# Start addresses in SBUF: 64 mod 512 for all against 0 mod 512 for most and 0, 32, 64 ... 480 for the split activations

## The chip, the cores and the metric

The kernel is one program on one NeuronCore of a Trainium2 chip. The metric is device time in microseconds (us) of one execution. Four compute engines matter: TensorE (PE in the profile; its weight loads are a row of their own, PEld), VectorE (DVE), ScalarE (ACT) and GpSimd (POOL). SyncE (SP) issues all of the kernel's transfers. Operands lie in SBUF, which has 128 partitions; an address is a byte offset in each partition, and a tile of 512 fp32 values takes 2048 bytes of it.

## The reference

One layer of a hybrid block on 512 latent tokens and 256 context tokens, model width 2048, all fp32:

```python
h = rmsnorm(x, g_norm1) * (1 + sc1) + sh1           # sc, sh, gt: c @ w_mod
lat_in, lat_gates = project_heads(h, w_in, ...)      # q, k, v of 4 GLA and 4 mLSTM heads, gates
ctx_in, _ = project_heads(hc, w_in, ...)             # k, v of the context
lat = scans in both directions, from the context's final states
x = x + gt1 * (concat(norm(gla) * silu(g), sigmoid(o) * norm(mlstm)) @ w_out)
h2 = rmsnorm(x, g_norm2) * (1 + sc2) + sh2
u_gate, u_val = split(h2 @ w_up)                     # 2048 -> 2 x 5504
x = x + gt2 * ((silu(conv3x3(u_gate)) * u_val) @ w_down)
out = rmsnorm(x, g_final)
```

## The kernel before, in words

All big products are done in three parts. `split` (L88) rounds an fp32 tile to a "high" tile of type float32r with ScalarE and takes the rest as a "low" tile with VectorE; `mm3` (L99) then issues three matmuls into one PSUM bank: high by high, high by low, low by high. Each matmul loads its 128 x 128 stationary operand anew, so the PE row and the PEld row of the profile have the same count.

The weights come by `load_split` (L155): a transfer of 256 rows by 512 columns into one of four `raw` buffers, then `split` into one of two `hi` and two `lo` buffers. Every 128 columns of such a buffer are 512 bytes, so all stationary slices of a buffer start at the same address mod 512.

The activations lie in 32 tiles of 512 columns, 16 high and 16 low ones, made by `acttile` (L136). They hold in turn the normed input (`hTh`, `hTl`), the merged heads (`yTh`, `yTl`), and the normed input of the MLP (`h2h`, `h2l`). The products of the MLP's middle layer lie in other tiles (`gh`, `gl`, L935), made in the pool `fp`.

The stages in order of time. First the modulation vectors and the first two heads (`project_first`, L308; the order of its matmuls is pinned). Then the heads, one after another (`project`, `gla`, `mlstm`): here the banks `a` get q and k with the weights stationary and 512 tokens moving (L269), v with 128 tokens stationary and 256 weight columns moving (L274), and the context's k and v with 384 weight columns moving (L279). Then the output gates (banks `ga`, L817), the output projection (`wo`, L867), and the MLP: `up_gate` and `up_val` (banks `ug`, `uv`) by blocks of 512 columns, and `down_block` (banks `dn`) between them, the last block as `dl` (L992) by halves of the tokens. `unit` (L169) issues `ga`, `wo`, `ug` and `uv`: for each pair of row blocks it goes over four column blocks, and for each over the two row blocks, with three matmuls each.

Every instruction's engine and order is set by the scheduling layer from the program; the change keeps the order of all engines as it is: 11423 rows on PE, 1868 on DVE, 1187 on ACT, 236 on POOL and 660 on SP are the same in both programs.

The pools are laid out one behind another in SBUF in the order in which they are opened, each tile padded to a multiple of 32 bytes, behind a scratch area for descriptors that GpSimd would generate (16384 bytes by default). Where that puts the operands of the large products, in bytes mod 512 of their start:

| tiles | before | after |
|---|---|---|
| `hi`, `lo` weights and the `raw` of pool `wraw` | 64 | 0 |
| `hTh`, `hTl`, `yTh`, `yTl`, `h2h`, `h2l` (32 tiles) | 64, all | 0 to 480 in steps of 32 |
| `gh`, `gl` | 160 | 0 |
| `hch`, `hcl` (split context, 1024 bytes each) | 0 | 0 |

After the change the high tiles of row blocks 0 to 15 start at 256, 320, 0, 64, 128, 192, 256, 320, 384, 416, 448, 480, 384, 416, 448 and 480, the low ones at 288, 352, 32, 96, 160, 224, 288, 352, 0, 32, 64, 96, 128, 160, 192 and 224 mod 512.

Of the kernel before, what the change touches and what calls it, by code (L numbers as in the profile page):

```python
# [11 lines left out]
F32 = mybir.dt.float32  # L12
# [6 lines left out]
P = 128  # L19
# [3 lines left out]
T = 512  # L23
# [17 lines left out]

# columns of the constants
C_ID, C_LS, C_US, C_SEG = (P * i for i in range(4))
# [26 lines left out]
def block_kernel(ctx: ExitStack, tc: tile.TileContext, a: dict, out: bass.AP):  # L70
# [32 lines left out]

# [1 line left out]
    keep = pool(ctx, "keep")  # L105
    cst = keep.tile([P, C_END], F32, name="cst")
    cols = keep.tile([P, 148], F32, name="cols")
    msk = keep.tile([P, len(LEVELS), P], U8, name="msk")
    csil = keep.tile([P, KT], F32, name="csil")
    modc = {n: keep.tile([P, KT], F32, name=f"mod{n}") for n in (2, 3, 4, 5)}  # L110
# [25 lines left out]
    def acttile(k, part, name):  # L136
        return actp.tile([P, T], F32R, name=name, tag=f"a{part}{k}")

    def rsqrt(v, t, o):
        """o = v ** -0.5 with one Newton step; t is scratch."""  # L140
        S.activation(t, v, AF.Ln)
        S.activation(o, t, AF.Exp, scale=-0.5)
        mul(t, o, o)
        mul(t, t, v)
        V.tensor_scalar(out=t, in0=t, scalar1=-0.5, scalar2=1.5, op0=ALU.mult, op1=ALU.add)
        mul(o, o, t)
# [3 lines left out]

# [1 line left out]
    fillers = []  # L152
# [16 lines left out]
    def unit(src, name, xh, xl, n=4):  # L169
        """n accumulators: transposed products of 128 n weight columns with all 512 tokens."""  # L170
        accs = [acc(f"{name}_{i}") for i in range(n)]
        for kp in range(KP):
            wh, wl = load_split(src[kp], f"{name}_{kp}", w=P * n)
            for i in range(n):
                for kk in range(2):
                    k = 2 * kp + kk
                    mm3(accs[i], wh[:, kk, P * i : P * i + P], wl[:, kk, P * i : P * i + P],
                        xh[k], xl[k], k == 0, k == KT - 1)
        return accs

# [1 line left out]
    def mod_load(region, n):  # L182
        """The weights of 256 columns of one region."""
        raws = []
        for q in range(4):
            raws.append((wraw if q == 3 else mraw).tile([P, 4, 256], F32, name=f"raw_m{region}_{n}_{q}", tag="raw"))
            nc.sync.dma_start(raws[q], a["w_mod1"][8 * region + n, q])
        return raws

    def mod_rows(region, n, raws):  # L190
        """[128, 256]: the products with c and c_ctx, each in four parts on four rows."""
        bank = psb(f"ps_m{region}_{n}")
# [10 lines left out]
    def mod_cols(region, n, bank, rows):  # L203
        """Their sums as columns of 128 entries, with what the norm and the modulation make of them."""
        pc = bank[:, 256:260].rearrange("p (b c) -> p b c", c=2)
# [12 lines left out]
    def mod_chunk(region, n, kp, parts):  # L218
        """256 rows of the 512 columns n of one region, weighed by c and added up on DVE and Pool."""
        name = f"m{region}_{n}_{kp}"  # L220
# [16 lines left out]
    def mod_end(region, n, parts):  # L237
        """The sums over the partitions: four columns of 128 entries."""
        po = parts[1]
# [9 lines left out]
    def mod_fillers(regions, lag):  # L249
        """The steps of these regions; a block's sums end lag steps after its last load."""  # L250
        for region in regions:
            for n in range(4):
                parts = []
                for kp in range(KP):
                    fillers.append(lambda r=region, n=n, kp=kp, p=parts: mod_chunk(r, n, kp, p))
                fillers.extend([lambda: None] * (lag - 1))
                fillers.append(lambda r=region, n=n, p=parts: mod_end(r, n, p))
# [3 lines left out]

# [1 line left out]
    def project_chunk(kp, wh, wl, o, g, first=0, last=KT - 1):  # L263
        """256 rows of w into bank g of a head: q, k, v of two token tiles (twice), k and v of a context tile (twice)."""
        ks = list(enumerate((2 * kp, 2 * kp + 1)))
# [17 lines left out]
    def project(h):  # L283
        """q, k transposed and v for the latent tokens, k and v for the context tokens."""
        banks = [acc(f"a{h}_{g}", BANKS[g]) for g in range(6)]
# [7 lines left out]
    def early_group(kp, g, w, sums):  # L293
        """One bank of head 1, whose sums stay in SBUF."""
        ps = psb(f"a1_{kp}_{g}", BANKS[g])
# [12 lines left out]
    def project_first():  # L308
        """Heads 0 and 1 while the modulation vectors come in."""
        banks = [acc(f"a0_{g}", BANKS[g]) for g in range(6)]  # L310
# [60 lines left out]

# [1 line left out]
    st_h = ExitStack()  # L373
    states = pool(st_h, "states")
    # rows 0-15: the low rank decay inputs, row 16: ones, rows 32-47: the mLSTM gates
    glr = states.tile([48, T + TC], F32, name="glr")
# [4 lines left out]
    negg = states.tile([36, T], F32, name="negg")  # L381
    bg = states.tile([36, 2], F32, name="bg")
    accp = pool(st_h, "accp")
# [4 lines left out]

    # head 1, first in the places of activations that come last, then of inputs that were used first
    EARLY = 4  # L390
# [33 lines left out]
    def stream_rstd(xs, o, name, n):  # L424
        """[128, n]: each token's 1 / rms, the same in all rows; xs are [128, 512], the tokens once or twice."""
        tot = xp.tile([P, T], F32, name=f"sq_{name}", tag="sqs")
# [44 lines left out]
    V.tensor_copy(msk, mskf)  # L471
    # decay inputs and gate inputs: 32 columns, partial sums over k = g mod 4 in four row groups
    V.memset(glr, 1.0)
# [19 lines left out]

# [1 line left out]
    st_2 = ExitStack()  # L495
# [33 lines left out]
    def finish(h, ob, ssq, yT):  # L529
        """Head norm, then transposed into the two channel tiles of the head."""  # L530
        var = wtile(f"var{h}", "st1", TJ)
# [14 lines left out]
    def gla(h, pair, qk, v, kn, vn, yT):  # L546
        wlr = wk.tile([17, 2, DK], F32, name=f"wlr{h}", tag="wlr")
        nc.sync.dma_start(wlr, a["w_lr"][h])
        # context: final states
        cla = ytile(13, f"cla{h}", (P, 2, CJ, DK))  # L550
# [24 lines left out]

        # latent: decays, cumulated within 128 tokens, and over all of them
        la = wtile(f"la{h}", "la", 2, T)
# [20 lines left out]

        # scores by levels: pairs of neighbouring spans of b tokens, both directions at once
        sc = wtile(f"sc{h}", "la", 2, TJ, P)  # L600
# [66 lines left out]
    def ml_gates():  # L667
        """Rows 0-3: forward, time as context, latent; rows 32-35: backward, time as latent, context."""
        W = T + TC
# [56 lines left out]
    def mlstm(h, _, qk, v, kn, vn, yT):  # L726
        hh = h - H
        q, k = qk
        # context: final states
        kt = ytile(15, f"kt{h}", (P, 2, CJ, DK))  # L730
# [5 lines left out]
        for d in range(2):  # L736
# [3 lines left out]
            S.copy(c0[:, d, :], ps)  # L740
        # latent
        qs = wtile(f"qs{h}", "tmp", 2, T)
# [67 lines left out]

# [1 line left out]
    st_3 = ExitStack()  # L812
# [12 lines left out]
    tc.keep_in_program_order(S.preload_act_table_set("natural_log_exp_and_others"))  # L825
# [1 line left out]
    yh, yl, x2 = [], [], []  # L827
# [10 lines left out]
    def square(k, sums, pl, tag, sl=slice(0, T)):  # L838
        """Adds the squares of x2[k] to the first of sums, or appends them for the last two."""
        n = sl.stop - sl.start  # L840
# [8 lines left out]
    def token_rstd(sums, pl, name, n=T):  # L849
        """[128, n] in PSUM: each token's 1 / rms, the same in all rows."""  # L850
        nj = n // P
# [36 lines left out]

# [1 line left out]
    fp = pool(ctx, "fp")  # L890
    tp = pool(ctx, "tp", 4)
    cwt = fp.tile([P, NF, 9], F32, name="cwt")
    cbt = fp.tile([P, NF], F32, name="cbt")
    nc.sync.dma_start(cwt, a["conv_w"])
# [70 lines left out]

# [1 line left out]
    tc.keep_in_program_order(S.preload_act_table_set("natural_log_exp_and_others"))  # L967
# [47 lines left out]
def arrange(x, c, ctx, c_ctx, w_mod, b_mod, g_norm1, g_norm2, w_in, gla_w_lr, gla_b_lr, mlstm_b_gate,  # L1015
            gla_g_norm, mlstm_g_norm, w_out, w_up, conv_w, conv_b, w_down, g_final):
    """The inputs in the layouts that the kernel reads: only moved, never computed with."""
    def col(v):
        return v.reshape(-1, P).T

    def blocks(w, n):
        """[K, n columns] -> [K / 256, 128, 2, n]."""
        return w.reshape(-1, 2, P, n).transpose(0, 2, 1, 3)
# [53 lines left out]
```

## Time and profile before

| | |
|---|---|
| median of 3 runs | 2644.12 us (2642.51 to 2647.18) |
| profiled execution, first to last instruction | 2643.6 us |
| PE busy | 2570.1 us, 12866 matmuls |
| PEld busy | 2136.7 us, 12866 loads |
| DVE, ACT, POOL busy | 1366.2, 860.2, 285.0 us |
| moved from and to HBM | 315.10 MB, 4.19 MB |

The profile has one execution, whose span is 2643.6 us; the profile gives no other time for it. Matmuls are pipelined: the duration of one in the profile (some 390 ns for 512 columns) is its way through the array, and overlaps with the next. What a matmul costs is the distance from its start to the start of the next, which is read from the chain that ended last (a length and a count) or from the starts in the timeline.

### The profile page before, as it was taken

The page shows a single profiled execution, that of the slowest core. Times are in us where ns is not written, and L with a number is a line of the kernel's source. Part 1 is how long each engine was busy: PE and PEld are TensorE (multiplying, and loading weights), DVE is VectorE, ACT ScalarE, POOL GpSimd, SP SyncE. Part 2 cuts the span into 40 slices and gives each one's busy share as a digit, 9 for nine tenths or more (in the row PEclk, how much of TensorE's full clock was granted, in tenths as well). Part 3 has the DMA queues.
Part 4 walks back from the last instruction along what each step waited for, and adds up shares of the span by engine and source line. Part 5 has one row for each costly group of instructions (what it writes and reads, how often), then busy time and mean ns, then how long its engine had stood idle before and what let it go on. Part 6 is the DMA issues. An engine that isn't in the chain of part 4 may idle for free.

```text
span 2643.6 us, 31995 instructions
## 1 busy us (share of the span) xinstructions
PE 2570.1 (97%) x12866; PEld 2136.7 (81%) x12866; DVE 1366.2 (52%) x1971; ACT 860.2 (33%) x1219; POOL 285.0 (11%) x255
## 2 busy tenths in 40 slices
PE   6999999999999999999999999999999999999998
PEld 4887888878987888887878888888888888888887
DVE  6656664554334465548686336533653365326534
ACT  4223433333323344334343123312331233123332
POOL 0002221302112232310331000000000000000001
PEclk9999999999999999999999999999999999999998
DMA  8750102213323566642554222222232223222323
GB/s 315 281 196 33 41 33 72 70 35 112 128 94 119 183 229 222 205 159 76 202 175 156 96 96 96 96 96 96 96 96 96 96 97 96 95 96 90 105 90 99
DMA packets 96348, 321.38 MB, mean 122 GB/s; under 512 B 10884, under 2 KB 15304, under 8 KB 96200
## 3 DMA queue, kind: packets, MB, share of 16 engines
q1 hardware_dynamic: 96200, 319.34, 35.4%
q8 instruction: 101, 1.65, 0.3%
q14 instruction: 47, 0.39, 0.0%
HBM read 315.10 MB, written 4.19 MB: 121 GB/s over the span
## 4 chain that ended last, share of the span: by engine, by line
PE 86%; DVE 7%; DMA 3%; ACT 2%; issue 2%; POOL 0%; SPq 0%; POOLq 0%; ACTq 0%; DVEq 0%
PE ug L95 17%; PE dn L95 17%; PE uv L95 16%; PE a L95 14%; PE wo L95 6%; PE ga L95 6%; DMA raw_m<-in_w_mod 2%; PE po L662 2%; PE po L782 1%; PE ps_m L95 1%; PE dl L95 1%; PE sl L631 1%; DVE ex L80 1%; DVE cv L924 1%; DVE ex L83 1%
## 5 line engine op out<-in xcount | busy, mean ns | idle before, releaser
L95 PE MATMUL ug<-h2h,hi_ug 128*128 128x512 f32 x688 | 269.0, 392 | 1.6 <-ACT h2h L883 1.6
L95 PE MATMUL uv<-h2h,hi_uv 128*128 128x512 f32 x688 | 268.7, 391 | 1.4 <-ACT hi_uv L89 1.4
L95 PE MATMUL uv<-h2h,lo_uv 128*128 128x512 f32 x688 | 268.6, 390 | 1.1 <-DVE lo_uv L90 1.1
L95 PE MATMUL ug<-h2h,lo_ug 128*128 128x512 f32 x688 | 268.6, 390 | 0.7 <-DVE lo_ug L90 0.7
L95 PE MATMUL ug<-h2l,hi_ug 128*128 128x512 f32 x688 | 268.6, 390 | 0.0
L95 PE MATMUL uv<-h2l,hi_uv 128*128 128x512 f32 x688 | 268.4, 390 | 0.0
L95 PE MATMUL dn<-gh,lo_d 128*128 128x512 f32 x644 | 256.9, 399 | 0.0
L95 PE MATMUL dn<-gl,hi_d 128*128 128x512 f32 x644 | 253.8, 394 | 0.0
L95 PE MATMUL dn<-gh,hi_d 128*128 128x512 f32 x644 | 252.5, 392 | 0.0
L924 DVE SCALAR_TENSOR_TENSOR cv<-pad,cwt,cv 128x512 f32<-128x512 f32 x344 | 242.2, 758 | 10.5 <-ACT cv L922 9.1
L233 POOL TENSOR_TENSOR sum_m<-sum_m,raw_m 128x512 f32<-128x512 f32 x112 | 174.2, 1555 | 552.4 <-ACT raw_m L232 304.8
L90 DVE TENSOR_TENSOR lo_ug<-raw_ug,hi_ug 128x1024 fp32r<-128x1024 f32 (+1 forms) x88 | 107.4, 1221 | 241.3 <-ACT hi_ug L89 241.3
L90 DVE TENSOR_TENSOR lo_uv<-raw_uv,hi_uv 128x1024 fp32r<-128x1024 f32 (+1 forms) x88 | 105.3, 1196 | 182.2 <-ACT hi_uv L89 181.8
L90 DVE TENSOR_TENSOR lo_d<-raw_d,hi_d 128x1024 fp32r<-128x1024 f32 x82 | 98.8, 1205 | 173.0 <-ACT hi_d L89 171.3
L231 DVE SCALAR_TENSOR_TENSOR sum_m<-raw_m,csil,sum_m 128x512 f32<-128x512 f32 x112 | 101.9, 910 | 151.8 <-DMA raw_m<-in_w_mod 148.1
L89 ACT CAST hi_d<-raw_d 128x1024 fp32r<-128x1024 f32 x82 | 84.9, 1035 | 291.2 <-PE dn L95 207.0
L89 ACT CAST hi_ug<-raw_ug 128x1024 fp32r<-128x1024 f32 (+1 forms) x88 | 90.8, 1032 | 267.8 <-PE ug L95 200.1
L89 ACT CAST hi_uv<-raw_uv 128x1024 fp32r<-128x1024 f32 (+1 forms) x88 | 90.9, 1033 | 254.7 <-PE uv L95 182.0
L95 PEld LDWEIGHTS uv<-h2h,lo_uv 128*128 128x128 f32 x688 | 129.6, 188 | 29.3 <-DVE lo_uv L90 2.3
L95 PEld LDWEIGHTS ug<-h2h,hi_ug 128*128 128x128 f32 x688 | 129.8, 189 | 29.0 <-ACT h2h L883 1.9
L95 PEld LDWEIGHTS uv<-h2h,hi_uv 128*128 128x128 f32 x688 | 129.4, 188 | 28.9 <-ACT hi_uv L89 1.8
L95 PEld LDWEIGHTS ug<-h2h,lo_ug 128*128 128x128 f32 x688 | 129.7, 189 | 28.3 <-DVE lo_ug L90 1.1
(310 smaller groups left out, 5277.6 us busy)
## 6 DMA issues: line engine op xcount, KB each, us to landing
raw_m<-in_w_mod SPq DMA_DIRECT2D x192, 512.0 KB, 4.3
raw_ug<-in_w_up SPq DMA_DIRECT2D x80, 512.0 KB, 3.2
raw_uv<-in_w_up SPq DMA_DIRECT2D x80, 512.0 KB, 3.2
raw_d<-in_w_down SPq DMA_DIRECT2D x79, 512.0 KB, 3.4
raw_h<-in_w_heads SPq DMA_DIRECT2D x64, 512.0 KB, 3.2
raw_ga<-in_w_gates SPq DMA_DIRECT2D x32, 512.0 KB, 3.7
raw_wo<-in_w_out SPq DMA_DIRECT2D x32, 512.0 KB, 3.7
xl<-in_xT SPq DMA_DIRECT2D x16, 256.0 KB, 5.4
```

The source lines that it names most:

```text
L80: V.tensor_tensor(out=o, in0=x, in1=y, op=ALU.subtract)
L83: V.tensor_tensor(out=o, in0=x, in1=y, op=ALU.mult)
L89: S.copy(hi, x)
L90: return V.tensor_tensor(out=lo, in0=x, in1=hi.bitcast(F32), op=ALU.subtract).ins
L95: ins = PE.matmul(*args, **kw)
L231: V.scalar_tensor_tensor(out=dv, in0=raw[:, 0, :], scalar=ce, in1=dv, op0=ALU.mult, op1=ALU.add)
L233: G.tensor_tensor(out=po, in0=po, in1=raw[:, 1, :], op=ALU.add)
L631: PE.matmul(ps[:, i, :], ex[:, 1, P * i : P * i + P], ex[:, 0, P * j : P * j + P], start=True, stop=True)
L662: PE.matmul(po, l, r, start=(n == 0), stop=(n == len(parts) - 1))
L782: PE.matmul(po, e[:, P * j - j0 : P * j - j0 + P], v[i], start=False, stop=(i == rng[-1]))
L924: V.scalar_tensor_tensor(out=t3, in0=src, scalar=w, in1=t3, op0=ALU.mult, op1=ALU.add)
```

## The change

The scratch area shrinks to 1024 bytes, and three small tiles (`csil`, `bg`, `cbt`) become longer, so that the tiles behind them start at multiples of 512 bytes. The 32 activation tiles become 2080 bytes long instead of 2048, of which 2048 are used as before, so that each starts 32 bytes further on, mod 512, than the one before it. The comments and doc strings that the diff also takes out do nothing and are left out here.

```diff
@@ block_kernel
-    csil = keep.tile([P, KT], F32, name="csil")
+    csil = keep.tile([P, 128], F32, name="csil")[:, 0:KT]
...
     def acttile(k, part, name):
-        return actp.tile([P, T], F32R, name=name, tag=f"a{part}{k}")
+        return actp.tile([P, T + 8], F32R, name=name, tag=f"a{part}{k}")[:, 0:T]
...
-    bg = states.tile([36, 2], F32, name="bg")
+    bg = states.tile([36, 24], F32, name="bg")[:, 0:2]
...
-    cbt = fp.tile([P, NF], F32, name="cbt")
+    cbt = fp.tile([P, 152], F32, name="cbt")[:, 0:NF]
@@ kernel
-    nc = bacc.Bacc("TRN2", target_bir_lowering=False, num_devices=1)
+    nc = bacc.Bacc("TRN2", target_bir_lowering=False, num_devices=1, dynamic_dma_scratch_size=1024)
```

## The prediction

> **What bounds the kernel now.** I read the page first (busy time, then the chain that ended last, as shares), then the chain in order of time, then the groups of instructions, and at last single matmuls in the timeline.
>
> ```profile
> span 2643.6 us, 31995 instructions
> PE 2570.1 (97%) x12866; PEld 2136.7 (81%) x12866; DVE 1366.2 (52%) x1971; ACT 860.2 (33%) x1219; POOL 285.0 (11%) x255
> ...
> PE 86%; DVE 7%; DMA 3%; ACT 2%; issue 2%; POOL 0%; SPq 0%; POOLq 0%; ACTq 0%; DVEq 0%
> ...
> raw_ug<-in_w_up SPq DMA_DIRECT2D x80, 512.0 KB, 3.2
> ```
>
> TensorE is busy for 97% of the span and is 86% of the chain, so the end moves with what a matmul costs. The chain in time shows that cost, block by block:
>
> ```profile
> 1510.00:2611.00 1101.00, 1101.00 (x4882) 905.91 (x4881) 513.34 (x623) 312.43 (x381) 0.00 (x0) 1.00 0.29 95
> ```
>
> ```profile
> 837.18 37.99 PE ga L95 x167
> ...
> 1123.69 43.63 PE wo L95 x192
> ...
> 1513.97 43.56 PE uv L95 x192
> 1557.54 43.52 PE ug L95 x192
> 1601.05 43.52 PE uv L95 x192
> 1644.57 43.52 PE ug L95 x192
> 1688.09 89.61 PE dn L95 x384
> ...
> 2593.47 17.88 PE dl L95 x149
> ```
>
> The first row is a window (length, then busy time and count of PE, PEld, DVE, ACT, POOL, clock, DMA): from 1510 to 2611 us PE is never idle, at a granted clock of 1.00, and DVE is busy for 513.34 of 1101 us. The chain rows (start, length, count) give the distance between matmuls: 43.52 / 192 = 226.7 ns in `ug` and `uv`, but 89.61 / 384 = 233.4 ns in `dn`, and 17.88 / 149 = 120.0 ns in `dl` with half as many columns. `ug` and `dn` run the same instruction at the same clock, three parts by `mm3`, 512 columns, with a weight load behind each start. What differs is where the operands begin: weights and activations both at 64 mod 512 in `ug`, the moving `gh` and `gl` at 160 against weights at 64 in `dn`. So 6.7 ns a matmul go with the address.
>
> How much can go with it at most? At half clock the same matmul shows no such loss:
>
> ```profile
> 1194.60:1199.28 4.68, 4.68 (x13) 3.62 (x12) 4.61 (x9) 1.63 (x2) 0.00 (x0) 0.50 0.00 0
> ```
>
> ```profile
> 1197.42 0.63 PE L95 MATMUL ug<-h2h,lo_ug 128*128 128x512 f32 x1
> 1197.84 0.63 PE L95 MATMUL ug<-h2h,hi_ug 128*128 128x512 f32 x1
> 1198.27 0.63 PE L95 MATMUL ug<-h2l,hi_ug 128*128 128x512 f32 x1
> ...
> 1513.81 0.40 PE L95 MATMUL uv<-h2h,hi_uv 128*128 128x512 f32 x1
> ...
> 1515.89 0.39 PE L95 MATMUL uv<-h2h,hi_uv 128*128 128x512 f32 x1
> 1516.12 0.39 PE L95 MATMUL uv<-h2l,hi_uv 128*128 128x512 f32 x1
> ```
>
> The first three starts, at clock 0.50, are 425 ns apart on average, half of which is 212.5 ns. At full clock a steady matmul takes 226.7, so some 14 ns are lost beside the stream of columns. The next rows are the first matmuls of `uv` behind a `dn` block: nine of them, from 1513.81 to 1515.89, take 2080 / 9 = 231.1 ns each, and only then does the distance become 226.7. I read this as two streams, the moving columns and the next weights, that need a few operations to settle into the order in which they disturb each other least; in `dn` they never reach it. It is a reading; the numbers stand without it.
>
> **The change part by part.** The order of instructions on each engine and on the queues of SP and POOL is unchanged, and so is every wait; only addresses move.
>
> Part 1, the smaller scratch area and the three longer small tiles. All transfers are issued on SP's queue (the issue row above names it), none by GpSimd, so nothing uses the scratch: no cost. What it does is to put weights, `raw`, `gh` and `gl` at 0 mod 512. For `dn` this makes moving and stationary starts equal, as they are in `ug` now, so I price a `dn` matmul at 226.7.
>
> ```profile
> L95 PE MATMUL dn<-gh,lo_d 128*128 128x512 f32 x644 | 256.9, 399 | 0.0
> L95 PE MATMUL ug<-h2h,hi_ug 128*128 128x512 f32 x688 | 269.0, 392 | 1.6 <-ACT h2h L883 1.6
> L95 PE MATMUL ga<-hTh,hi_ga 128*128 128x512 f32 x256 | 100.9, 394 | 0.0
> L95 PE MATMUL wo<-yTh,hi_wo 128*128 128x512 f32 x256 | 100.0, 391 | 0.0
> L95 PE MATMUL a<-hTh,hi_h 128*128 128x512 f32 x256 | 104.3, 408 | 2.4 <-ACT hTh L89 1.6 <-ACT qk L513 0.7
> ```
>
> Each count is one of the three parts of `mm3`. `dn` has 3 x 644 = 1932 matmuls, nearly all of them on the chain (its rows of 384 and its zero idle time): 1932 x 6.69 ns = 12.9 us less. Its ends are 0 (if the 233.4 has another cause) and 12.9.
>
> Part 2, the staggered activations. They are the moving operand of 3 x 688 in each of `ug` and `uv` (4128), 3 x 256 in each of `ga` and `wo` (1536) and 3 x 256 in `a` (768). These now start anywhere in steps of 32 against weights at 0. Which offsets cost? The rows give three: 0 (`ug`, 226.7), 96 (`dn`, 233.4), and 64, in the context's products of 384 columns (weights move at 64 mod 512, `hch` and `hcl` stand at 0):
>
> ```profile
> 297.05 0.34 PE L95 MATMUL a<-lo_h,hch 128*128 128x384 f32 x1
> ...
> 298.09 0.34 PE L95 MATMUL a<-lo_h,hch 128*128 128x384 f32 x1
> ```
>
> Six of them take 1040 / 6 = 173.3 ns; 384 columns at 212.5 / 512 ns are 159.4, so the loss is 14 ns, the same as at offset 0. With three points the plainest rule is that an even multiple of 32 costs as 0 does and an odd one as 96 does. By that rule one matmul in three is odd in row blocks 0 to 7 (high, low, high at a, a + 32, a), and one in two in blocks 8 to 15 (there both tiles of every second block are odd): 5/12 in the mean, 5/12 x 6.69 = 2.8 ns. Against it stands that the offset now changes from one matmul to the next, and that a changed sequence needs nine matmuls to settle: if it never settles, all pay the 231.1 of the unsettled nine, 4.4 ns more. I take the middle, 3.6 ns, with 2.8 and 4.4 as the forecast's own ends; the outer ends are 0 (it settles as now) and 6.7 (all pay as `dn`).
>
> How many lie on the path? `ug` and `uv` all (the window above has no idle PE, and before it they are the largest pieces), `ga` and `wo` all but a few gaps, and of `a` I count half, 384, since between the heads' steps PE waits for other engines and a slower matmul only eats idle time. 4128 + 1536 + 384 = 6048; x 3.6 ns = 21.8 us more.
>
> Part 3, the same tiles as stationary operands of the 256-column products of `a`, and `dl`, whose weights lie in activation tiles:
>
> ```profile
> 295.04 0.28 PE L95 MATMUL a<-lo_h,hTh 128*128 128x256 f32 x1
> ...
> 296.00 0.28 PE L95 MATMUL a<-hi_h,hTh 128*128 128x256 f32 x1
> ```
>
> Eight of them take 960 ns, 120.0 each at offset 0; `dl` takes 120.0 at offset 96. With 256 columns the offset costs nothing, so I put 0 here, with bounds of 3 ns either way on half of 3 x 512: 2 us.
>
> Part 4, everything else that moves: VectorE, ScalarE and GpSimd read and write the same tiles at other addresses. Were they slower by a tenth, DVE would still be busy for some 565 of the 1101 us above: the cover is its idle half, and it would have to go before the end moved. Transfers land at other offsets in SBUF; a load of 512 KB lands in 3.2 us, one of 256 KB in the row below in 2.6,
>
> ```profile
> raw_d<-in_w_down SPq DMA_DIRECT2D x3, 256.0 KB, 2.6
> ```
>
> so 64 bytes out of 4096 can be worth some 0.6 x 2 / 64 = 0.02 us a load, and DMA is 3% of the chain: under 1 us either way.
>
> Sum: -12.9 + 21.8 = +8.9 us, a span of 2652.5. The profiled execution's span lies 0.5 us under the median of the runs, 2644.12, so I predict 2653 us.
>
> [...]
>
> **The rivals.**
>
> A, not slower: the staggered streams settle as they do now, at 226.7, since the shift of 32 bytes is small against 2048, and only `dn` changes. 2644.1 - 12.9 = 2631 us. For it: offsets 0 and 64 both settle at a loss of 14 ns. Against it: the nine unsettled matmuls of `uv`. It decides from a price under 12.9 / 6048 = 2.1 ns on.
>
> B, the change does nothing: the pace depends on something else than addresses, such as the loop order of `down_block`; then both terms are 0 and the time is 2644 us. For it: only two stages are compared. Against it: the same instruction, clock and operand count in both. [...]
>
> C, worse: every staggered matmul pays the 6.7 ns of `dn`: 6048 x 6.69 = 40.5, less 12.9, is 2672 us; or the price is as forecast and `dn` keeps its 233.4, 2644.1 + 21.8 = 2666. For it: `dn` never settles at an odd offset.
>
> D, the stagger takes the collisions away: half of the 14 ns gone on 6048 matmuls is 42 us, with `dn` 55: 2589 us. For it: 14 ns are there to be had. Against it: no steady stage of this trace has lost less, at offsets 0, 64 or 96.
>
> **How the numbers follow.** About 0.2%, 5.3 us, is what a measurement of this kernel can tell from no change. Chances: the forecast 0.55 (from 6048 x 2.8 - 12.9 = +4.0 to 6048 x 4.4 - 12.9 = +13.7, so 2648 to 2658; 0.08 of it within 0.2%), A 0.17, B 0.08, C 0.15, D 0.05. Faster is A and D, 0.22; same B and the lower end of the forecast, 0.16; slower the rest, 0.62. The range takes in A with its 2 us of part 3 and C with the same on top: 2629 to 2676, leaving out D and what of C is worse than `dn`'s price.
>
> **What would show it.** In the chain after, `dn` rows of 384 should be 87.0 us (226.7 each), and `ug` and `uv` rows of 192 between 44.0 and 44.4; `dl` and the 256-column starts should stay at 120 ns. Rows of 43.5 mean A, `dn` rows still at 89.6 mean B or C's second form, rows over 44.8 C, rows under 43 D. The prediction is wrong if the price goes by more than the offset mod 64, or if a few misplaced matmuls set off a longer unsettled stretch than nine.

## The result, and the profile after

The changed kernel takes 2658.97 us in the median of 4 runs (2657.11 to 2660.06), the kernel before 2644.85 (2642.51 to 2647.18) beside it: a ratio of 1.0046, with a 95% interval of 1.0031 to 1.006. It is slower, by 0.3 to 0.6%. All times of the block here are of executions at a granted clock near 0.99; two far slower ones, one of `gh` moved below (4295.86 us at a clock of 0.556) and one of the kernel before (8361.22 us), are left out. The profiled execution has grown by 11.5 us, from 2643.6 to 2655.1.

The page of the kernel after (span, busy time, shares of the chain that ended last):

```profile
span 2655.1 us, 31995 instructions
PE 2584.2 (97%) x12866; PEld 2136.1 (80%) x12866; DVE 1362.3 (51%) x1971; ACT 861.0 (32%) x1219; POOL 283.6 (11%) x255
...
PE 86%; DVE 7%; DMA 2%; ACT 2%; issue 2%; POOL 0%; SPq 0%; POOLq 0%; ACTq 0%; DVEq 0%
```

TensorE is as busy a share as before, with the same 12866 matmuls in 14.1 us more. The chain of the kernel after in order of time (start, length, what, count):

```profile
836.70 38.81 PE ga L95 x167
...
1127.80 44.63 PE wo L95 x192
...
1519.60 44.53 PE uv L95 x192
1564.13 44.54 PE ug L95 x192
...
1697.75 87.08 PE dn L95 x384
...
2605.47 17.64 PE dl L95 x149
```

`dn` has fallen to 87.08 / 384 = 226.8 ns a matmul, what `ug` took before. `ug` and `uv` have risen from 226.7 to 44.54 / 192 = 232.0, and `wo` by the same (44.63 against 43.63 us for 192). `dl`, with 256 columns, went from 120.0 to 118.4.

Where the 11.5 us arose is read by laying the starts of the same steps side by side. Two pairs of rows are missing for it, the sums of the norm ahead of the MLP (`ps_rms`) and the first block of the MLP; here is the same view of the kernel before,

```profile
1186.16 2.41 PE ps_rms L855 x20
...
1193.84 46.56 PE ug L95 x192
```

and of the kernel after:

```profile
1191.60 3.93 PE ps_rms L855 x20
...
1200.81 47.09 PE ug L95 x192
```

| stretch, by the starts of its rows | before, us | after, us | difference |
|---|---|---|---|
| start to the first long row of `ga` | 837.18 | 836.70 | -0.48 |
| from there to the first `ug` (gates, output projection) | 356.66 | 364.11 | +7.45 |
| from there to the `uv` behind the first `dn` | 320.13 | 318.79 | -1.34 |
| from there to `dl` (steady MLP) | 1079.50 | 1085.87 | +6.37 |
| from there to the end | 50.13 | 49.63 | -0.50 |

In the steady MLP the paces give the difference: the rows there count 3168 matmuls of `ug` and `uv` at +5.31 ns (+16.8 us) and 1548 of `dn` at -6.59 (-10.2). In the two stretches ahead of it the granted clock has a part. From the first long row of `ga` to the last start of `wo` the kernel takes 5.9 us more (346.98 and 352.92), where 1536 matmuls at +5.2 ns would give 8.0; the other 1.5 us of the 7.45 lie behind `wo`, where the clock had already dropped when `ps_rms` ran: its 20 matmuls took 3.93 us at a clock of 0.58 after, and 2.41 at 1.00 before.

From the first `ug` to the `uv` behind the first `dn` the paces would give 960 x 5.31 - 2.5 = +2.6 us, and the stretch became 1.3 shorter, 3.9 less than that. Windows at half clock make up some half of it (length, busy time and count of PE, clock, share and GB/s of the DMA), before

```profile
1193.84:1199.70 5.86, 5.86 (x14) 0.50 0.00 0
1366.90:1370.30 3.40, 3.40 (x9) 0.51 0.80 239
```

and after:

```profile
1200.81:1205.80 4.99, 4.99 (x12) 0.50 0.00 0
```

At half clock a matmul takes 425 ns in place of 227 or 232, so 9.3 us of it against 5.0 are some 2.0 us. Whether the change has to do with this stays open: of all the traces, the second of these windows is missing in those with steps of 32 and 64 and in that of `gh` moved alone, and is there in the others. The rest, some 1.9 us, are for the most part waits of PE that are gone. In the timeline before, the matmuls at 1290.47 and 1358.70 us wait for a low tile of the weights and start 1.04 and 0.95 us after the one ahead of them; such waits do not occur there after.

### The profile page after: what moved, and what is told of

Same layout as the page of the kernel before. It is cut to its first block, busy times and chain, and to the rows that moved or that the text cites. A ratio compares the mean times of both kernels' runs of the same rounds, so it can differ in the third digit from the quotient of the medians.

```text
span 2655.1 us, 31995 instructions
## 1 busy us (share of the span) xinstructions
PE 2584.2 (97%) x12866; PEld 2136.1 (80%) x12866; DVE 1362.3 (51%) x1971; ACT 861.0 (32%) x1219; POOL 283.6 (11%) x255
## 4 chain that ended last, share of the span: by engine, by line
PE 86%; DVE 7%; DMA 2%; ACT 2%; issue 2%; POOL 0%; SPq 0%; POOLq 0%; ACTq 0%; DVEq 0%
PE ug L95 18%; PE uv L95 17%; PE dn L95 17%; PE a L95 13%; PE wo L95 7%; PE ga L95 6%; PE po L662 2%; DMA raw_m<-in_w_mod 1%; PE po L782 1%; PE ps_m L95 1%; PE dl L95 1%; DVE ex L80 1%; PE sl L631 1%; DVE ex L83 1%; DVE cv L924 1%
## 5 line engine op out<-in xcount | busy, mean ns | idle before, releaser
L95 PE MATMUL dn<-gh,lo_d 128*128 128x512 f32 x644 | 250.5, 389 | 0.0
```

Source lines behind the costliest of these rows:

```text
L95: ins = PE.matmul(*args, **kw)
```

## The experiments

My theory after the result was that the pace of a float32r matmul is set by where its moving operand begins against its stationary one, and that the two parts of the change act separately. The rivals were that the order of the work in `down_block` set the pace of `dn`, that only odd multiples of 32 cost (the prediction's rule), and that it is the change of the start from one matmul to the next that costs.

**Part 1 alone.** The layout of the change, with the activation tiles as before, all at 0 mod 512.

```diff
-        return actp.tile([P, T + 8], F32R, name=name, tag=f"a{part}{k}")[:, 0:T]
+        return actp.tile([P, T], F32R, name=name, tag=f"a{part}{k}")
```

> Part 1 alone: the changed kernel with the 32 activation tiles at 2048 bytes again, so weights, activations and the MLP's middle tiles all start at 0 mod 512. Theory (what counts is where moving and stationary operands start against each other, the prediction's part 1): the dn products go from 233.4 to 226.7 ns a matmul as in the changed kernel, ug and uv stay at 226.7: 2644 - 12.9 = about 2631 us. Rival (the whole layout, the smaller scratch area or the longer small tiles do something else): 2644 or more, or dn rows that differ from those of the changed kernel.

2634.34 us (2632.99 to 2634.68), ratio 0.9952 (0.9936 to 0.9967). Its chain:

```profile
1514.88 43.52 PE uv L95 x192
...
1688.96 87.04 PE dn L95 x384
```

`dn` is repaired and `ug` and `uv` keep 226.7: this part is worth some 13 us.

**Part 2 alone.** The kernel before with the longer activation tiles and the small scratch area.

```diff
-        return actp.tile([P, T], F32R, name=name, tag=f"a{part}{k}")
+        return actp.tile([P, T + 8], F32R, name=name, tag=f"a{part}{k}")[:, 0:T]
...
-    nc = bacc.Bacc("TRN2", target_bir_lowering=False, num_devices=1)
+    nc = bacc.Bacc("TRN2", target_bir_lowering=False, num_devices=1, dynamic_dma_scratch_size=1024)
```

> Part 2 alone: the kernel before with the 32 activation tiles 32 bytes longer each, and a scratch area of 1024 bytes to make room, which moves all else by a multiple of 512. Theory: ug, uv, ga and wo go from 226.7 to 232.0 as in the changed kernel, dn stays at 233.4: 2644 + 24 = about 2668 us (4128 + 1536 matmuls by 5.3 ns = 30 at most, less what lies beside other waits). Rival (the loss in the changed kernel comes from weights at 0 and not from the stagger): ug and uv stay at 226.7, 2644 us.

2671.4 us (2669.09 to 2672.03), ratio 1.0091 (1.0075 to 1.0107). Its chain:

```profile
1566.71 44.54 PE ug L95 x192
...
1700.33 89.60 PE dn L95 x384
```

`ug` pays the 232.0 of the change, `dn` its old 233.3. The two ratios, -0.48% and +0.91%, add up to +0.43%, beside the +0.46% of the whole: within the intervals, of some 0.15% to either side, the parts are independent.

**A constant difference of 32.** Weights at 0, all 32 activation tiles at 32 mod 512, none changing from one matmul to the next.

```diff
     wlo = pool(ctx, "wlo", 2)
+    shift = pool(ctx, "shift").tile([P, 8], F32, name="shift")
+    G.memset(shift, 0.0)
     actp = pool(ctx, "actp")
+    fill = pool(ctx, "fill").tile([P, 120], F32, name="fill")
+    G.memset(fill, 0.0)
...
-        return actp.tile([P, T + 8], F32R, name=name, tag=f"a{part}{k}")[:, 0:T]
+        return actp.tile([P, T], F32R, name=name, tag=f"a{part}{k}")
```

> The aligned layout, but all 32 activation tiles start at 32 mod 512: one constant offset instead of sixteen. Offset theory (each matmul pays by its own offset, odd multiples of 32 as dn did): ug and uv at 233.4, about 2631 + 5664 x 6.7 ns = 2669 us. Settling theory (a constant offset always settles, and only a changing one stays unsettled): ug and uv near 226.7, about 2631 us.

2668.9 us (2664.09 to 2670.31), ratio 1.0078 (1.0057 to 1.0099). Its chain:

```profile
1572.60 44.80 PE ug L95 x192
```

44.80 / 192 = 233.3 ns, the pace that `dn` had in the kernel before, now in `ug`, whose loop order is untouched. A start that never changes costs more than the stagger does.

**The pace by the offset, first table.** A small kernel with blocks of 96 matmuls in the order of `unit`; `A` is one long tile of activations, `mov` gives the byte in it at which the moving operand begins, `w` is where the weights begin, here in columns of 4 bytes:

```python
for kp in range(4):
    for i in range(4):
        for kk in range(2):
            k = 2 * kp + kk
            for part in range(3):
                m = mov(k, int(part == 1)) // 4
                s = (wh if part < 2 else wl)[:, w + 512 * kk + P * i : w + 512 * kk + P * i + P]
                tc.keep_in_program_order(PE.matmul(accs[i], s, A[:, m : m + n], start=(k == 0 and part == 0),
                                                   stop=(k == 7 and part == 2)))
```

> The disputed cost by itself; nothing of the block is computed, and what it writes is no result. 45 blocks of 96 matmuls each, the same three-part loop, the same weights and column counts, differing only in where the operands start: constant offsets of 0 to 480 (m), the weights moved instead (w), both moved alike (b), a step from tile to tile (s), high and low tiles at two places (h), 256 and 384 columns (n, t), and the changed kernel's own starts (real). Offset theory: 226.7 ns at even multiples of 32, 233.4 at odd ones, the same for m32 and w32, 226.7 in b32, and for the changing ones a mean by their share of odd offsets: s64 and h64 at 226.7, s32 and h32 between. Settling theory: every constant offset near 226.7 or 233.4, every changing one, s64 and h64 too, near 231 to 232. Rival D of the prediction (some offsets avoid the collision): a block under 222 ns.

Its chain, a row a block. The names: `m` moving operand alone shifted by so many bytes, `w` weights alone, `b` both, `s` a step from tile to tile, `n` as `m` with 256 columns, `t` with 384, `real` the starts of the changed kernel (here those of row blocks 0 to 7).

```profile
52.13 21.76 PE m0x L110 x96
...
96.13 22.40 PE m32x L110 x96
...
140.93 21.98 PE m64x L110 x96
162.91 22.41 PE m96x L110 x96
...
274.99 21.76 PE m256x L110 x96
...
453.21 22.39 PE w32x L110 x96
475.60 22.40 PE w64x L110 x96
...
564.03 21.81 PE b96x L110 x96
...
608.10 22.18 PE s64x L110 x96
...
652.67 21.78 PE s256x L110 x96
...
784.67 11.51 PE n0x L110 x96
...
807.50 11.31 PE n64x L110 x96
...
830.32 16.64 PE t0x L110 x96
...
897.20 22.30 PE realxa L110 x96
```

21.76 / 96 = 226.7 ns at a difference of 0 and of 256; 229.0 at 64; 233.3 at 32 and 233.4 at 96. Shifting both by 96 costs nearly nothing (21.81), so what counts is the difference of the two starts, mod 256: in the same table 288 gives 22.40 us as 32 does, and 320 gives 21.98 as 64 does. It has a sign: weights shifted by 64 (233.3) do not cost what a moving operand shifted by 64 does, but what one shifted by 256 - 64 = 192 does (22.39 us in the same table). A step of 256 changes the start at each tile and is free (21.78), a step of 64 is not (231.0). So both theories miss: the offset theory at 64 and at the step of 64, where it had 226.7, and the settling theory at the step of 256, where it had 231 to 232. The changed kernel's own starts give 232.3 here, beside 232.0 in the kernel itself.

**Steps of 64 and of 256 in the kernel.** The changed kernel with other lengths of the activation tiles.

```diff
-        return actp.tile([P, T + 8], F32R, name=name, tag=f"a{part}{k}")[:, 0:T]
+        return actp.tile([P, T + 16], F32R, name=name, tag=f"a{part}{k}")[:, 0:T]
```

> The changed kernel with the activation tiles 64 bytes longer each instead of 32, so they start at 0, 64, 128 ... 448 mod 512, all even multiples of 32. The prediction's rule (odd multiples of 32 cost, even ones do not): ug and uv at 226.7, about 2634 us as with all tiles aligned. Theory after the first runs (what counts is the start of the moving operand against that of the weights mod 256, and only 0 is free): ug and uv near the 231.1 ns of the block with a step of 64 bytes, 2634 + 5664 x 4.4 ns = about 2659 us.

2659.24 us (2657.02 to 2660.02), ratio 1.005 (1.0033 to 1.0066), the time of the change itself. Its chain:

```profile
1567.53 44.49 PE ug L95 x192
```

All starts are even multiples of 32 here, and the matmul still takes 231.7 ns. With `T + 64`, a step of 256 bytes:

> The changed kernel with the activation tiles 256 bytes longer each, so their starts alternate between 0 and 256 mod 512. Theory (mod 256): ug and uv at 226.7, about 2634 us. Rival (a start that changes from matmul to matmul costs by itself, or the period is 512): ug and uv at 231 to 232, about 2660 us.

2633.48 us (2632.88 to 2634.7), ratio 0.9954 (0.9939 to 0.9969), the time of part 1 alone. Its chain:

```profile
1557.70 43.52 PE ug L95 x192
```

So the start may change from tile to tile at no cost, as long as it changes by 256.

**`gh` moved alone.** The kernel before, with `cbt` 160 bytes longer. All tiles behind `cbt` move with it; of the operands of the large products these are `gh` and `gl` alone. The edit was run twice.

```diff
-    cbt = fp.tile([P, NF], F32, name="cbt")
+    cbt = fp.tile([P, NF + 40], F32, name="cbt")[:, 0:NF]
```

> The kernel before with one edit: 160 bytes more in front of the MLP's middle tiles, which puts gh and gl at 320 mod 512, that is 256 past the weights' 64; nothing is aligned to 512. Theory (difference mod 256): dn from 233.4 to 226.7, all else as before, 2644 - 12.9 = 2631 to 2634 us, as much as the whole aligned layout. Rival (starts must be multiples of 512 or 256 themselves): no change, 2644 us.

2629.76 us (2629.06 to 2629.87), ratio 0.9939 (0.9922 to 0.9955).

> The kernel before with 160 bytes in front of gh alone, once more for a trace of it: by the theory of the difference of the starts, dn rows of 384 at 87.0 us in place of 89.6, ug and uv rows of 192 at 43.5 as before, and a time 11 to 16 us under the kernel before. If instead the earlier gain came from elsewhere, the dn rows stay at 89.6.

2632.67 us (2631.39 to 2634.12), ratio 0.9943 (0.993 to 0.9956). The chain of the second:

```profile
1555.94 43.52 PE ug L95 x192
...
1686.51 87.04 PE dn L95 x384
...
2581.38 17.87 PE dl L95 x149
```

All of part 1's gain is `dn`'s: the weights still begin at 64 mod 512, and only the difference to `gh` and `gl` has become a multiple of 256. This one line is faster than both kernels of the case.

**The pace by the offset, second table.** Finer steps, more points for 256 and 384 columns, and plain fp32.

> A second run of blocks of 96 matmuls, nothing of the block computed. Constant offsets between those of the first (4 to 252), more of them for 256 and 384 columns, and two blocks of plain fp32 instead of float32r (f0, f96). Theory (mod 256): 104 to 240 near 233, no block of 512 columns under 226; s192, s224, s320 and h192 near 231 to 232, as they change. Rival D of the prediction: an offset between the tried ones at which the collision is gone, under 222. For plain fp32, which takes two passes at half the data rate, both theories expect no difference between f0 and f96, as at half clock.

Its chain (`f` is plain fp32 with 256 columns, which shows as two instructions each; the other names as above):

```profile
75.12 22.86 PE m4x L113 x96
...
365.92 21.76 PE m240x L113 x96
...
512.06 10.89 PE n192x L113 x96
...
751.90 41.44 PE f0x L113 x192
793.34 41.45 PE f96x L113 x192
```

A shift of 4 bytes already costs 11 ns (238.1), and 240 is a second free place, where the expectation had 233. With 512 columns nothing in either table is below 226.7, as expected. With 256 columns equal starts are among the slowest (119.9): 96 costs the same, 113.4 at 192 is the lowest, and the other places tried in the two tables lie between 117 and 119. Plain fp32 does not see the offset: 215.8 ns an instruction at 0 and at 96.

**The good place for 256 columns, in the kernel.** Part 1 with the stationary operands of the 256-column products 64 bytes further on, so that the difference is 192 mod 256.

```diff
-    def acttile(k, part, name):
-        return actp.tile([P, T], F32R, name=name, tag=f"a{part}{k}")
+    def acttile(k, part, name, off=0):
+        return actp.tile([P, T + 64], F32R, name=name, tag=f"a{part}{k}")[:, off : off + T]
...
-        hi = whi.tile([P, n, w], F32R, name=f"hi_{name}", tag="hi")
+        hi = whi.tile([P, 1088], F32R, name=f"hi_{name}", tag="hi")[:, off : off + n * w]
...
-                hx[0].append(acttile(k, "h", f"hTh{k}"))
+                hx[0].append(acttile(k, "h", f"hTh{k}", 16))
...
-        accs = unit(a["w_gates"][g], f"ga{g}", *hx)
+        accs = unit(a["w_gates"][g], f"ga{g}", *hx, off=16)
...
-        wh, wl = acttile(n, "h", f"dlh{f}"), acttile(n, "l", f"dll{f}")
+        wh, wl = acttile(n, "h", f"dlh{f}", 16), acttile(n, "l", f"dll{f}", 16)
```

> Edit: the layout of the big buffers of the change, the 32 activation tiles made 256 bytes longer (all still begin at multiples of 256), and the transposed h, the split weights of the gates ga and the left factors of dl begin 64 bytes into their tiles. So each 256-column product of stage a and of dl has its moving operand 192 bytes past its stationary one, mod 256, where the second micro kernel took 10.89 us for 96 matmuls (113.3 ns) against 11.50 (119.8) at 0; ga has both operands moved alike; the products q and k of stage a have a difference of 64, where the micro kernels took 228.8 ns against 226.7. The theory that only the difference of the two starts mod 256 sets the pace: the 256-column rows near 10.9 us for 96, that is 113 ns for each of some 1,536 in stage a and 264 in dl, an estimate of 10.2 + 1.8 = 12 us less of TensorE's busy time, about 1.5 us back on q and k; against the aligned layout's 2634.3 us some 2624 to 2630 us, since part of stage a waits for loads; the ug, uv and dn rows stay at 43.5 and 87.0 us. Rival, that the gain at 192 belongs to the micro kernel's regular blocks: the 256-column rows stay near 120 ns and the time at 2634 to 2636.

2631.07 us (2626.11 to 2634.91), ratio 0.9934 (0.9922 to 0.9946): not to be told from `gh` moved alone, measured beside it (0.9943, to 0.9956). By the distance of their starts in the timeline, the 256-column products of `a` take 119.5 ns in the mean in part 1 alone and 116.7 here. That mean is made of two paces. Two stretches of 24 such products, 5 us apart and with the same starts:

```profile
683.85 0.28 PE L95 MATMUL a<-hi_h,hTl 128*128 128x256 f32 x1
...
685.55 0.28 PE L95 MATMUL a<-hi_h,hTl 128*128 128x256 f32 x1
...
690.50 0.28 PE L95 MATMUL a<-hi_h,hTh 128*128 128x256 f32 x1
...
693.21 0.28 PE L95 MATMUL a<-hi_h,hTl 128*128 128x256 f32 x1
```

15 steps from the first to the second row are 113.3 ns each, 23 from the third to the fourth 117.8. Of the 52 unbroken stretches of 16 or more such products in `a` and `dl`, 14 end at 113.3 and 38 at 117.8; in part 1 alone they end near 120. The long row of `dl` in the chain is one of the slower ones,

```profile
2581.34 17.55 PE dl L95 x149
```

117.8 ns, and the `dl` stretch of 58 behind it, from 2602.27 on, goes at 113.3.

The expectation missed: the mean pace of `a` moved the right way by 2.8 ns, less than half of the table's 6.4. 1536 x 2.8 ns are some 4 us, and the time shows no more than that. For 256 columns the difference mod 256 isn't the whole rule in the kernel: at one difference there are two paces that last. How a stretch begins goes with them. Of these 52 stretches 40 come right behind a product of 512 columns; in 33 the first start lies 224 to 227 ns behind that product's, and all of these end at 117.8, in 7 it lies 231 to 236 ns behind, and all of these end at 113.3. That this decides it was not tried.

**What the loss is made of.** A third small kernel: fewer stationary columns, and a close look around 192.

> A micro kernel: it computes nothing of the block, but times 96 matmuls for each pair of starts. First, 512 moving columns against 128, 96, 64 and 32 stationary columns, at a difference of 0 and of 96 bytes. If what a matmul takes beyond 512 cycles is a collision of the moving operand's reads with those of the next weight load, it goes with the size of that load: at 0, 21.76 us for 128 columns and near 20.5 for 32, and at 96, 22.4 falling likewise. Rival, a fixed gap between matmuls: 21.76 and 22.4 at every width. Second, 256 moving columns at differences of 176, 184, 192, 200 and 208: a low at 192 alone (10.89) or a wide one. With both operands moved by 192, 11.5 as at 0 if only the difference counts. Third, 128 moving columns at 0, 64 and 192.

Its chain (`c` stationary columns and `o` the difference, `v` both operands shifted, `k` 128 moving columns; `n` as before):

```profile
51.88 21.76 PE c128o0x L113 x96
73.64 22.41 PE c128o96x L113 x96
...
140.31 22.08 PE c64o0x L113 x96
162.40 22.22 PE c64o96x L113 x96
...
240.69 11.52 PE n184x L113 x96
252.21 10.90 PE n192x L113 x96
263.12 11.52 PE n200x L113 x96
...
286.07 11.51 PE v192x L113 x96
297.58 10.67 PE k0x L113 x96
```

Both expectations of the first table fail. A half as large stationary operand does not halve the loss: at a difference of 0 it costs more (230.0 against 226.7), at 96 less (231.5 against 233.4). So the loss does not go with the size of the weight load, and is no fixed gap either; what the difference of the starts costs shrinks from 6.8 ns to 1.5. The best place for 256 columns is 192 alone, 8 bytes to either side take 120.0 again, and with both operands moved by 192 it is gone: there too it is the difference that counts. What inside TensorE or SBUF makes the difference of the starts matter stays open.

## Why the prediction was right, and where its steps failed

The forecast was 2653 us in a range of 2629 to 2676, slower at 0.62; 2658.97 lies in the range and just above the forecast's own 2648 to 2658. The direction and the first part are right in their mechanism. That the sum comes within 6 us is in part luck, since two errors of the second part work against each other. The upper end of the range is 2 us above what the text adds up (2671.7 + 2), which changes nothing here.

**The bound** held: TensorE is 97% busy and the end moved with the pace of its matmuls.

**Part 1** held in size and in cause. The forecast had -12.9 us at 226.7; the rows give 226.8, and 2.5 + 10.2 = 12.7 us. Moving `gh` alone gave all of it.

**Part 2** is the term that was mis-sized, in two ways that partly cancel. The step "an even multiple of 32 costs as 0 does and an odd one as 96 does" is wrong: a difference of 64 costs 2.3 ns by itself, a step of 64 costs 5 in the kernel, and of the multiples of 32 only 0 mod 256 is free. The three points that I had could not tell this, and the one for 64 came from products of 384 columns, where 64 is free: 173.3 ns in the trace of before, the same as 16.64 / 96 at 0 in the first table. I carried it to 512 columns, where it is not. The other end, 4.4 ns from the nine unsettled matmuls, was the better one, and 5.3 lies above it. The middle, 3.6 ns, was two thirds of the price. The rows show it against the prediction's own signs: `ug` and `uv` at 44.54 us for 192 lie over the 44.0 to 44.4 that it named, and the price does go "by more than the offset mod 64", namely by the difference mod 256.

The count failed the other way. The 3168 of the steady MLP were all there. Of the 8.0 us of `ga` and `wo` 2.1 went into waits that became shorter, of the 5.1 us of the first blocks of the MLP some 1.9; "`ug` and `uv` all" overlooked that PE still waits for weights there. In stage `a` there was little to pay: its rows of 6 to 12 products with 512 columns do not reach 226.7 before either, so that by their starts they rose from 229.9 to 232.2 ns only, 768 x 2.3 = 1.8 us, while the 1536 products with 256 columns fell from 119.5 to 118.1, 2.2 us. The term came out at 11.5 + 12.7 = 24.2 us, where 6048 x 5.31 would be 32.1 and the forecast had 21.8: a price a third too low on a count a third too high. The half-clock windows of the two profiled executions (+1.5 and -2.0 us) stand in the 24.2 as well, and part 2 alone, 0.91% of 2644.85, gives 24.1.

**The reading of the nine matmuls**, two streams that need some operations to settle, is supported in part: starts that change by 32 or 64 stay at 231 to 232 throughout, and even with equal starts the first ten matmuls of block `b96x` lie 224 to 236 ns apart before 226.7 lasts. But the cause is not the change, since a step of 256 is free and a constant 32 costs more in the kernel than any step tried.

**Part 3** held in its sum and not in its rule. The whole stretch up to `ga` moved by 0.5 us, inside the bound of 2. But "with 256 columns the offset costs nothing" is wrong: 0 and 96 happen to be equal (119.9), while 32 and 64 give 117.8 and 192 gives 113.4; `dl` went to 118.4, not 120, and the 2.2 us that `a` gained offset what its 512-column products lost.

**Part 4** held: DVE is busy for 1362.3 us against 1366.2, and its share of the chain is 7% in both.

**The rivals.** A, all settled at 226.7, is what the step of 256 does, not the step of 32. B, that addresses do not matter, fell with the 160 bytes in front of `gh`, and with 226.7, 233.3 and 238.1 ns for the same matmul at differences of 0, 32 and 4. C's first form is what a constant 32 gives (2668.9, forecast 2672), and its second form is part 2 alone (2671.4, forecast 2666). D found nothing: no pair of starts tried for 512 columns is faster than equal ones.

## What to carry to other kernels

When TensorE is the bound and a row of matmuls is a few ns slower than another of the same shape, compare where both operands begin: in float32r here, equal starts mod 256 were worth 6.6 ns of 233. For 512 columns aligning every buffer alike kept the best pace and staggering them did not, and a padding of 160 bytes in front of one tile gained about as much (0.6%) as the whole rearrangement lost (0.5%). Measure the pace per offset and per width before carrying one to another: 384 columns were free at 64, where 512 were not, and with 256 columns equal starts were among the slowest. A pace from a regular block is not sure to hold in a kernel, either: 113.4 at 192 became 116.7 in the mean.

## What the runs showed of the hardware

- The pace of a float32r matmul with 512 columns is 226.7 ns for starts that differ by 0, 240 or 256 bytes, 229.0 for 64, 233.3 for 32, 233.4 for 96, and 238.1 for 4. It goes by the difference of the starts, moving less stationary: both shifted by 96 give 227.2, and weights shifted by 96 give 234.2, as a moving operand shifted by 160 does. Its period is 256: 229.0 at 320 as at 64, 233.3 at 288 as at 32.
- With equal starts the time beside the columns is the same at three widths: 226.7, 173.3 and 119.9 ns for 512, 384 and 256 columns (21.76, 16.64 and 11.51 us for 96) are 0.417 ns a column and 13.3 ns more. With 128 columns it is not: 111.1 ns (10.67 us for 96) are 58 more than the columns. With 256 columns and a difference of 192 half of the 13.3 goes in the small kernels; in the block two paces occur there, 113.3 and 117.8 ns.
- Plain fp32 shows no such effect: 215.8 ns an instruction of 256 columns at both offsets. Each of its matmuls shows as two such instructions, where float32r takes one, of 119.9 ns at equal starts. No float32r block here with 512 columns came below 226.7.
